# A two-layer encoder trunk in split fp32: low parts of two x forms made by DMA, a swapped pair of copies, an earlier weight split

## The chip, the cores and the metric

The kernel runs on one core of a Trainium2 chip. The metric is the device time of one execution in microseconds (us), as the median of several runs. Smaller is better. The engines are named as the profile names them: PE (matrix products; PEld is its weight loading), DVE (vector), ACT (scalar), POOL (GpSimd), SP (which here only starts transfers). Sixteen DMA engines move data for all queues; the profile calls the queue of transfers started by POOL q0 and the queue of those started by SP q1.

## The reference

Two layers run over x of 512 rows and 1024 columns. Each layer is a half-step SwiGLU FFN (hidden width 2816), a mixer, a second such FFN, and a gated embedding; each of these ends in a residual and a layer norm. The mixer of layer 0 is an mLSTM, that of layer 1 a gated MLP.

```
for i in range(DEPTH):
    x = layer_norm(DN_ALPHA*x + 0.5*swiglu_ffn(x, ffn1_wgu[i], ffn1_wd[i]), ...)
    x = layer_norm(DN_ALPHA*x + mixer(x), ...)          # mLSTM for i == 0, gMLP for i == 1
    x = layer_norm(DN_ALPHA*x + 0.5*swiglu_ffn(x, ffn2_wgu[i], ffn2_wd[i]), ...)
    x = layer_norm(DN_ALPHA*x + sigmoid(x @ ple_wg[i] + ple_bg[i]) * (p[i] @ ple_wp[i]), ...)

def swiglu_ffn(x, w_gu, w_d):
    g, u = split(x @ w_gu, 2); return (silu(g) * u) @ w_d
```

All inputs are float32, and the changed parts belong to `x @ w_gu` of the four FFNs and to the step from an FFN to the mixer behind it.

## The kernel before, in words

**Split products.** Every float32 operand is split in two fp32r tiles: a high part (the rounded value) and a low part (value minus high part). A product is three matmuls, high by high, high by low, low by high (`mm3`, L396, L397, L398 in the profile). So each weight tile passes ACT once for its high part (`whi`, L281), and its low part (`wlo`) is made in one of two ways:

- by DVE, as source minus high part (L290 or L296);
- by DMA: ACT writes the rounded value with its sign turned into the low tile (L287), and POOL starts a transfer that adds the source to it in place (L288, "DMA" `wlo<-wbox`). Both read the source; neither needs the high part.

**Seven products for eight.** Large products are done by a Strassen-like scheme. For the up projection of an FFN (`up_forms` for the weights, `UpForms` for x) four quarters of a pair of weight column blocks give seven weight forms, and the quarters of x give seven right-hand forms. The forms are numbered from 0 in the code and called first to seventh here. The fifth weight form (`s3`) and the third (`s2`) are sums that DVE makes in place in the loaded tile (L143 to L152); they are in the set `W.sums`. Which weight forms get their low part by DMA is in `UP_BY_DMA = (1, 3, 4, 5, 6)` for the first pair of each chunk, and in shorter lists for a chunk's second pair and for the last chunk. The fifth form (index 4) is in the first list only.

Of x, four forms are quarters as they stand and three are new: `t2` for the third product, `t1` for the fourth and `t4` for the seventh. A fourth sum, `t3`, replaces a quarter of x in place (the tiles `xh`, `xl`) and is used by the fifth product. `t2` already gets its low part by DMA. `t1`, `t3` and `t4` get theirs from DVE.

**Chunks.** An FFN's 22 hidden blocks run in chunks of 2, 4, 4, 4, 4 and 4 blocks. The first four blocks are plain products (`fps`, `sup`); the first pair by seven products is the second half of chunk 1. While its products run (`up_products`), the remaining x forms are made from the table `self.last`, one entry after each product: 0 splits `t3`, 1 and 2 make `t4`, 3 makes its high part, 4 its low part. After every second up product comes one product of the down projection (`gps`).

**What sets the order.** Each engine does its instructions in the order in which this code issues them. SP starts weight loads (L243) as soon as a raw tile comes free, that is when the last reader of the tile, often the transfer of a low part, is done. `W.fill` splits the next weights of a list when there is a free pair of tiles. `W.hold` keeps it from splitting a weight whose load was started less than two products ago; `W.limit` keeps it from going past the end of the FFN.

**The end of an FFN.** The down product of the last blocks (`down`, `dps`) runs over four blocks of 128 rows, with residual and norm behind each. PE transposes the finished rows of x (`xps`, L649), and ACT scales and splits them (`xf` L654, `xh` L657, low part on DVE L658; `turn_x`). Two blocks of rows are transposed within the next stage, between its first products (`sup`, `up_staged`, L888 and L892), which go over three weight tiles.

Of the kernel before, what the change touches and what calls it, by code (L numbers as in the profile page):

```python
# [10 lines left out]
F32 = mybir.dt.float32  # L11
F32R = mybir.dt.float32r
AF = mybir.ActivationFunctionType
OP = mybir.AluOpType
# [36 lines left out]
class Weights:  # L51
# [199 lines left out]
    def fill(self, most=1000, low=None, meanwhile=None):  # L251

        while most and self.next_split < len(self.order) and self.next_split != self.limit:
            kind, js, make = self.order[self.next_split]
            if not self.free.get(kind):
                return meanwhile
            for j in js or ():
                while j not in self.raws:
                    if not self.load(self.loads[j][1]):
                        return meanwhile  # L260
                if self.hold and self.ready and self.loaded_at[j] > self.clock - 2:
                    return meanwhile
            if self.ahead and not self.forced and make in self.sums and make not in self.made:
                return meanwhile
            shape = [P, 2, 512]
            if js is not None:
                while any(m not in self.formed for m in self.after.get(make, ())):
                    self.lows(1)
                src, used = self.made.pop(make, None) or make()
                shape = list(src.shape)  # L270
            hi = self.pools[kind].tile(shape, F32R, name="whi", tag="whi")
            lo = self.pools[kind].tile(shape, F32R, name="wlo", tag="wlo")
            self.free[kind] -= 1
            self.next_split += 1
            if js is None:
                make(hi, lo)
                continue
            parts = 2 if self.next_split == 1 else 1
            for i in range(parts):
                s = slice(i * shape[1] // parts, (i + 1) * shape[1] // parts)  # L280
                self.nc.scalar.activation(hi[:, s], src[:, s], AF.Copy)  # L281
                if meanwhile and make in self.in_place:
                    meanwhile()
                    meanwhile = None
                if make in self.by_dma or low == "dma" and make not in self.in_place:

                    self.nc.scalar.activation(lo[:, s], src[:, s], AF.Copy, scale=-1.0)  # L287
                    self.nc.gpsimd.dma_start(lo[:, s], src[:, s], accum_op=OP.add)  # L288
                elif not self.apart:
                    self.nc.vector.tensor_sub(lo[:, s], src[:, s], hi[:, s].bitcast(F32))  # L290
            self.ready.append((kind, (hi, lo)))
            most -= 1

            def done(make=make, used=used, src=src, hi=hi, lo=lo, late=self.apart and make not in self.by_dma):
                if late:
                    self.nc.vector.tensor_sub(lo, src, hi.bitcast(F32))  # L296
                self.formed.add(make)
                for j in used:
                    self.left[j] -= 1
                while self.load():  # L300
                    pass

            if self.apart and make not in self.by_dma:
                self.pending.append((lo, done))
            else:
                done()
        return meanwhile
# [58 lines left out]
def hybrid_trunk(ctx: ExitStack, tc, x, p, ln_g, ln_b, ffn1_wgu, ffn1_wd, ffn2_wgu, ffn2_wd,  # L366
# [3 lines left out]
    nc = tc.nc  # L370
# [21 lines left out]
    vec, sca, pool = nc.vector, nc.scalar, nc.gpsimd  # L392
# [7 lines left out]
    def split(hi, lo, src):  # L400
        sca.activation(hi, src, AF.Copy)
        vec.tensor_sub(lo, src, hi.bitcast(F32))
# [46 lines left out]
    W = Weights(nc, raw_pool, split_pool)  # L449
# [562 lines left out]
    class UpForms:  # L1012


        def __init__(self, pool, late):
# [3 lines left out]
            b, c = f32(pool, "f1"), f32(pool, "f0")  # L1019
# [7 lines left out]
            def f32r(to, at, tag):  # L1027
                to.append(at.tile([P, 4, 256], F32R, name="t_" + tag, tag=tag))
                return to[-1]
# [13 lines left out]
            def split_t1():  # L1043
                both = act.tile([P, 2, 4, 256], F32R, name="t1", tag="gb")
                self.t1.extend((both[:, 0], both[:, 1]))
                for i, s in enumerate(halves):
                    split(self.t1[0][:, s], self.t1[1][:, s], a[i])

            def split_t2():
                hi, lo = f32r(self.t2, late, "whi"), f32r(self.t2, late, "wlo")  # L1050
                sca.activation(lo, c, AF.Copy, scale=-1.0)
                nc.gpsimd.dma_start(lo, c, accum_op=OP.add)
                sca.activation(hi, c, AF.Copy)

            self.steps = [
                x22, lambda: joined(b, 0, 1), t3, lambda: joined(c, 0, 0), lambda: vec.tensor_add(c, b, c),
                split_t2, t1, split_t1]

            d = [tmp.tile([P, 2, 256], F32, name="x_d", tag="pad", bufs=3) for _ in range(2)]
# [14 lines left out]
            def t4_low():  # L1074
                lo = f32r(self.t4, pool, "f0")
                for i, s in enumerate(halves):
                    vec.tensor_sub(lo[:, s], d[i], self.t4[0][:, s].bitcast(F32))

            self.last = {0: lambda: split(*self.t3, b), 1: x21, 2: t4, 3: t4_high, 4: t4_low}
            self.right = [self.quarter(0, 0), self.quarter(1, 0), self.t2, self.t1, self.t3,  # L1080
                          self.quarter(1, 1), self.t4]

# [55 lines left out]
    def ffn(layer, k, rows, late, prepare=None):  # L1138
        with stage_pool("forms", 2) as fpool, stage_pool("quarters", Q_BUFS) as qpool, \
# [58 lines left out]
            for c, n in enumerate(FFN_CHUNKS):  # L1198
# [36 lines left out]
                else:  # L1235
# [3 lines left out]
                        next_group.form()  # L1239
                    group.add()  # L1240
                    group = next_group
            W.limit = None
            W.fill()
            W.apart, W.ahead, W.hold = (layer, k) == (0, 0), False, False
            return down(hs, False, norm, lazy=layer == 0, defer=prepare is not None)

    def ffn_stage(layer, k):
        with stage_pool("rows", 2) as rows, stage_pool("late") as late:
            W.open("rows", rows, 2)
            ffn(layer, k, rows, late)  # L1250
            W.close("rows")
            W.close("rowsx")
# [573 lines left out]
    def ffn_ple(i, last):  # L1826
        with stage_pool("rows", 2) as rows, stage_pool("late") as late:
# [3 lines left out]
            def load_p():  # L1831
# [13 lines left out]
                turn_p.append(turn)  # L1845

            finish = ffn(i, 2, rows, late, load_p)
            with stage_pool("extra", PLE_EXTRA) as extra, stage_pool("rows2") as rows2, stage_pool("ple2") as mp:
                W.open("extra", extra, PLE_EXTRA)
# [123 lines left out]
```

## Time and profile before

| | us |
|---|---|
| median of three runs (2177.74 to 2182.6) | 2177.97 |
| the profiled execution | 2179.46 |
| its span, first to last instruction | 2177.8 |
| PE busy in the span | 2161.0 |
| DVE busy | 1761.4 |
| ACT busy | 1244.9 |
| POOL busy | 253.8 |

The span is what the profile's rows add up to; the execution has 1.7 us more around it. The profiled execution is 1.5 us above the median. Busy shares are averages over stages that differ, and PE's busy time is that of pipelined matmuls, so the waits of PE, and what ended them, are read beside them.

### The profile page before, as it was taken

The numbers are of one execution on the slowest core, as the hardware profiler recorded it, in microseconds if no ns is written. First come the engines' busy times: TensorE is split into PE (matmuls) and PEld (weight loads), VectorE is DVE, ScalarE is ACT, GpSimd is POOL, SyncE is SP. The second block draws the span as 40 slices with busy tenths as digits, with TensorE's granted clock in tenths as the row PEclk, the third lists the DMA queues.
The fourth block names the chain that finished last, engine by engine and source line by source line (L and its number), as shares of the span: only waits on it lengthen the run. The fifth ranks groups of instructions, "written<-read, shape, count | busy, mean of one in ns | idle before, by whom it ended". The sixth has DMA issues, their size and how long they took to land. (4 is left out here: it accounts for less than half of the span.)

```text
span 2177.8 us, 33285 instructions
## 1 busy us (share of the span) xinstructions
PE 2161.0 (99%) x13109; PEld 1931.7 (89%) x13109; DVE 1761.4 (81%) x2540; ACT 1244.9 (57%) x1712; POOL 253.8 (12%) x311
## 2 busy tenths in 40 slices
PE   9999999999999999999999999999999999999998
PEld 8999998888888889999988999998888888999987
DVE  6988887777776789888887988887788678888897
ACT  4766656464646456666445666655345556666542
POOL 1111101011101111111000111100011101111100
PEclk9999999999999999999999999999999999999999
DMA  7887763366847468787544887763338748877651
GB/s 216 195 196 189 172 169 115 88 152 135 160 123 155 126 160 199 193 203 166 149 131 128 205 200 186 173 166 122 128 78 155 160 129 214 186 192 176 137 173 59
DMA packets 232836, 346.28 MB, mean 159 GB/s; under 512 B 9780, under 2 KB 164532, under 8 KB 232680
## 3 DMA queue, kind: packets, MB, share of 16 engines
q0 software_dynamic: 56832, 117.64, 31.8%
q1 hardware_dynamic: 169232, 211.83, 30.2%
q10 hardware_dynamic: 6616, 14.69, 2.0%
q8 instruction: 103, 1.69, 0.3%
q14 instruction: 53, 0.43, 0.1%
HBM read 224.58 MB, written 2.11 MB: 104 GB/s over the span
## 5 line engine op out<-in xcount | busy, mean ns | idle before, releaser
L281 ACT ACTIVATE whi<-wbox 128x1024 fp32r<-128x1024 f32 x252 | 265.1, 1054 | 239.9 <-DVE wbox L144 95.2
L398 PE MATMUL ups<-xh,wlo 128*128 128x256 f32 x1152 | 326.5, 283 | 4.3 <-DMA wlo<-wbox 4.3
L397 PE MATMUL ups<-xl,whi 128*128 128x256 f32 x1152 | 325.9, 283 | 0.0
L396 PE MATMUL ups<-xh,whi 128*128 128x256 f32 x1152 | 325.7, 283 | 0.0
L396 PE MATMUL gps<-whi,fhi 128*128 128x512 f32 x644 | 252.9, 393 | 0.0
L281 ACT ACTIVATE whi<-wraw 128x1024 fp32r<-128x1024 f32 (+1 forms) x196 | 200.5, 1045 | 90.8 <-DVE wraw L121 22.6
L397 PE MATMUL gps<-wlo,fhi 128*128 128x512 f32 x644 | 252.3, 392 | 0.0
L398 PE MATMUL gps<-whi,flo 128*128 128x512 f32 x644 | 251.5, 390 | 0.0
L288 POOL DMA_DIRECT2D wlo<-wbox x160 | 135.6, 848 | 945.5 <-ACT wlo L287 572.9
L398 PEld LDWEIGHTS ups<-xh,wlo 128*128 128x128 f32 x1152 | 220.7, 192 | 5.2 <-DMA wlo<-wbox 5.1
L397 PEld LDWEIGHTS ups<-xl,whi 128*128 128x128 f32 x1152 | 220.6, 192 | 2.6
L396 PEld LDWEIGHTS ups<-xh,whi 128*128 128x128 f32 x1152 | 220.6, 192 | 2.6
L784 DVE TENSOR_TENSOR xt<-xt,gps 128x512 f32<-128x512 f32 x302 | 195.6, 683 | 28.4 <-PE gps L398 28.3
L290 DVE TENSOR_TENSOR wlo<-wraw,whi 128x1024 fp32r<-128x1024 f32 (+1 forms) x120 | 143.5, 1213 | 38.1 <-ACT whi L281 37.2
L281 ACT ACTIVATE whi<-wquarter 128x1024 fp32r<-128x1024 f32 (+1 forms) x140 | 135.2, 966 | 56.4 <-ACT wlo L287 20.2
L287 ACT ACTIVATE wlo<-wbox 128x1024 fp32r<-128x1024 f32 x160 | 167.1, 1044 | 0.0
L398 PEld LDWEIGHTS gps<-whi,flo 128*128 128x128 f32 x644 | 120.9, 188 | 27.0
L396 PEld LDWEIGHTS gps<-whi,fhi 128*128 128x128 f32 x644 | 121.3, 188 | 22.0
L397 PEld LDWEIGHTS gps<-wlo,fhi 128*128 128x128 f32 x644 | 121.4, 188 | 21.3
L296 DVE TENSOR_TENSOR wlo<-wquarter,whi 128x1024 fp32r<-128x1024 f32 (+1 forms) x116 | 139.3, 1201 | 0.0
L970 DVE TENSOR_TENSOR flo<-h,fhi 128x512 fp32r<-128x512 f32 (+1 forms) x140 | 88.8, 637 | 44.6 <-ACT fhi L967 44.5
L967 ACT ACTIVATE fhi<-h 128x512 fp32r<-128x512 f32 (+1 forms) x140 | 80.4, 574 | 47.6 <-DVE h L1220 28.7
(367 smaller groups left out, 5814.7 us busy)
## 6 DMA issues: line engine op xcount, KB each, us to landing
wlo<-wbox POOLq DMA_DIRECT2D x160, 512.0 KB, 5.9
wbox<-in_ffn_wgu_dram SPq DMA_DIRECT2D x144, 512.0 KB, 4.6
wquarter<-in_ffn_wd_dram SPq DMA_DIRECT2D x64, 512.0 KB, 6.5
wraw<-in_ml_w_in_dram SPq DMA_DIRECT2D x24, 1024.0 KB, 5.7
wlo<-wraw POOLq DMA_DIRECT2D x48, 512.0 KB, 6.6
wraw<-in_gm_w_in_dram SPq DMA_DIRECT2D x15, 1024.0 KB, 5.9
wraw<-in_ffn_wgu_dram SPq DMA_DIRECT2D x17, 512.0 KB, 4.5
wraw<-in_ffn_wd_dram SPq DMA_DIRECT2D x8, 1024.0 KB, 5.0
```

Source lines behind the costliest of these rows:

```text
L281: self.nc.scalar.activation(hi[:, s], src[:, s], AF.Copy)
L287: self.nc.scalar.activation(lo[:, s], src[:, s], AF.Copy, scale=-1.0)
L288: self.nc.gpsimd.dma_start(lo[:, s], src[:, s], accum_op=OP.add)
L290: self.nc.vector.tensor_sub(lo[:, s], src[:, s], hi[:, s].bitcast(F32))
L296: self.nc.vector.tensor_sub(lo, src, hi.bitcast(F32))
L396: mm(ps, st[0], mv[0], start=start, stop=False, skip_group_check=more)
L397: mm(ps, st[0], mv[1], start=False, stop=False, skip_group_check=more)
L398: mm(ps, st[1], mv[0], start=False, stop=stop, skip_group_check=more)
L784: vec.tensor_add(dst, dst, ps)
L967: sca.activation(hi, src, AF.Copy)
L970: vec.tensor_sub(lo, src, hi.bitcast(F32))
```

## The change

There are four parts.

1. The low part of `t3` comes by DMA: ACT writes the negated copy into `xl`, POOL starts the adding transfer, then ACT writes `xh`. The DVE subtraction goes. A new helper `split_by_dma` does this for `t2` and `t3`.
2. The low part of `t4` comes by DMA too, in two halves, and is issued one entry earlier in the table (with the high part, after the fourth product). The two DVE subtractions go.
3. For a weight form that is a sum and whose low part comes by DMA (only the fifth form, in the first pair of each chunk), the negated copy and its transfer are issued before the high part.
4. `W.hold` is cleared before the `W.fill()` at the end of an FFN instead of after it.

```diff
+                by_dma = make in self.by_dma or low == "dma" and make not in self.in_place
+
+                def negated():
+                    self.nc.scalar.activation(lo[:, s], src[:, s], AF.Copy, scale=-1.0)
+                    self.nc.gpsimd.dma_start(lo[:, s], src[:, s], accum_op=OP.add)
+
+                if by_dma and make in self.sums:
+                    negated()
                 self.nc.scalar.activation(hi[:, s], src[:, s], AF.Copy)
...
-                if make in self.by_dma or low == "dma" and make not in self.in_place:
-
-                    self.nc.scalar.activation(lo[:, s], src[:, s], AF.Copy, scale=-1.0)
-                    self.nc.gpsimd.dma_start(lo[:, s], src[:, s], accum_op=OP.add)
-                elif not self.apart:
+                if by_dma and make not in self.sums:
+                    negated()
+                if not by_dma and not self.apart:
                     self.nc.vector.tensor_sub(lo[:, s], src[:, s], hi[:, s].bitcast(F32))
...
+            def split_by_dma(hi, lo, src):
+                sca.activation(lo, src, AF.Copy, scale=-1.0)
+                nc.gpsimd.dma_start(lo, src, accum_op=OP.add)
+                sca.activation(hi, src, AF.Copy)
+
             def split_t2():
-                hi, lo = f32r(self.t2, late, "whi"), f32r(self.t2, late, "wlo")
-                sca.activation(lo, c, AF.Copy, scale=-1.0)
-                nc.gpsimd.dma_start(lo, c, accum_op=OP.add)
-                sca.activation(hi, c, AF.Copy)
+                split_by_dma(f32r(self.t2, late, "whi"), f32r(self.t2, late, "wlo"), c)
...
             def t4_low():
                 lo = f32r(self.t4, pool, "f0")
                 for i, s in enumerate(halves):
-                    vec.tensor_sub(lo[:, s], d[i], self.t4[0][:, s].bitcast(F32))
-
-            self.last = {0: lambda: split(*self.t3, b), 1: x21, 2: t4, 3: t4_high, 4: t4_low}
+                    sca.activation(lo[:, s], d[i], AF.Copy, scale=-1.0)
+                    nc.gpsimd.dma_start(lo[:, s], d[i], accum_op=OP.add)
+
+            self.last = {0: lambda: split_by_dma(*self.t3, b), 1: x21, 2: t4, 3: lambda: (t4_high(), t4_low())}
...
-            W.limit = None
+            W.limit, W.hold = None, False
             W.fill()
-            W.apart, W.ahead, W.hold = (layer, k) == (0, 0), False, False
+            W.apart, W.ahead = (layer, k) == (0, 0), False
```

How this moves instructions: PE's and SP's rows keep their order. DVE loses three subtractions in each FFN, twelve in all.

ACT after the first up product of the second FFN, before the change. `us` is the copy of that product, `x_f` the tile of `t3`, the first `whi`, `wlo` are the fifth weight form, the second pair the sixth:

```order
L1114 ACTIVATE us<-ups 128x512
L401 ACTIVATE xh<-x_f_7664 128x4x256
L281 ACTIVATE whi<-wbox 128x1024
L287 ACTIVATE wlo<-wbox 128x1024
L281 ACTIVATE whi<-wbox 128x1024
L287 ACTIVATE wlo<-wbox 128x1024
```

The same place with the change (lines have moved: L284 is now the negated copy, L289 the high part):

```order
L1123 ACTIVATE us<-ups 128x512
L1056 ACTIVATE xl<-x_f_7667 128x4x256
L1058 ACTIVATE xh<-x_f_7667 128x4x256
L284 ACTIVATE wlo<-wbox 128x1024
L289 ACTIVATE whi<-wbox 128x1024 x2
L284 ACTIVATE wlo<-wbox 128x1024
```

A copy for `xl` has come in ahead of everything, and the fifth form's negated copy stands where it stood in the row, third after `us`; the sixth form's stands one copy later.

POOL from the end of the mLSTM stage to the end of the second FFN, before. The `wlo<-wbox` are the low parts of weight forms:

```order
L751 TENSOR_TENSOR rs<-rs,eps_pow 128x1 x4
L775 DMA xt<-gb 128x1024 x3
L288 DMA wlo<-wbox 128x1024
L775 DMA xt<-gb 128x1024
L1052 DMA t_wlo<-x_f_7665 128x1024
L288 DMA wlo<-wbox 128x1024 x39
L751 TENSOR_TENSOR rs<-rs,eps_pow 128x1 x8
```

With the change:

```order
L757 TENSOR_TENSOR rs<-rs,eps_pow 128x1 x4
L781 DMA xt<-gb 128x1024 x3
L285 DMA wlo<-wbox 128x1024
L781 DMA xt<-gb 128x1024
L1057 DMA t_wlo<-x_f_7668 128x1024
L285 DMA wlo<-wbox 128x1024
L1057 DMA xl<-x_f_7667 128x4x256
L285 DMA wlo<-wbox 128x1024 x3
L1086 DMA t_f_8137<-x_d 128x512 x2
L285 DMA wlo<-wbox 128x1024 x35
L757 TENSOR_TENSOR rs<-rs,eps_pow 128x1 x8
```

The transfer for `xl` has come in before those of the fifth, sixth and seventh weight form, and the two for `t4` (`t_f`) behind these three, ahead of the low part of the next chunk's second form.

ACT in the first products of the mLSTM stage, before. `xf` and `xh` are the last rows of x being turned, `whi` weights of the mLSTM, `pad` the first result of the stage:

```order
L654 ACTIVATE xf<-xps,cols 128x128 x4
L657 ACTIVATE xh<-xf 128x4x128
L281 ACTIVATE whi<-wraw 128x1024 x4
L654 ACTIVATE xf<-xps,cols 128x128 x4
L657 ACTIVATE xh<-xf 128x4x128
L654 ACTIVATE xf<-xps,cols 128x128 x4
L657 ACTIVATE xh<-xf 128x4x128
L1365 ACTIVATE pad<-sup,cols 128x512
```

With the change:

```order
L660 ACTIVATE xf<-xps,cols 128x128 x4
L663 ACTIVATE xh<-xf 128x4x128
L660 ACTIVATE xf<-xps,cols 128x128 x4
L663 ACTIVATE xh<-xf 128x4x128
L660 ACTIVATE xf<-xps,cols 128x128 x4
L663 ACTIVATE xh<-xf 128x4x128
L289 ACTIVATE whi<-wraw 128x1024 x3
L1374 ACTIVATE pad<-sup,cols 128x512
```

The four weight splits that stood ahead of the last two turned halves of x have left this place: one was done in the FFN's down product, three come behind the turned halves. The DVE low part of that one weight goes with it. At the start of the gMLP stage one of two such splits moves to the earlier place in the same way.

## The prediction

> **What bounds the kernel now.** I read the page first, then who PE waited for.
>
> ```profile
> span 2177.8 us, 33285 instructions
> PE 2161.0 (99%) x13109; PEld 1931.7 (89%) x13109; DVE 1761.4 (81%) x2540; ACT 1244.9 (57%) x1712; POOL 253.8 (12%) x311
> ...
> PEclk9999999999999999999999999999999999999999
> ...
> PE ups L398 <- DMA wlo<-wbox: 4.3, 4, 1.7
> ```
>
> PE is busy all but 17 us of the span, at full clock. So no change that leaves PE's work alone can gain more than about 0.7%, while what makes PE wait costs its whole length. The only repeated wait of PE is for low parts of weights that come by DMA, four times. They lie where this change works. The PE timeline of the second FFN and, as the fourth of them, of the last FFN:
>
> ```profile
> 822.50 0.39 PE L398 MATMUL ups<-xh,wlo 128*128 128x256 f32 x1 [0.70 <-DMA wlo<-wbox]
> 1852.10 0.39 PE L398 MATMUL ups<-xh,wlo 128*128 128x256 f32 x1 [0.53 <-DMA wlo<-wbox]
> ```
>
> The first is the fifth product (its matmul would have started 0.87 us earlier at the even step of 0.12 us), the second is the second product of the next chunk. Why these come late is seen in stretches of the second FFN. The last two columns are the DMA engines' busy share and GB/s:
>
> ```profile
> core 0: us, PE busy (x) PEld busy (x) DVE busy (x) ACT busy (x) POOL busy (x), PEclk, DMA share, GB/s
> ...
> 813.00:815.00 2.00, 2.00 (x13) 1.74 (x13) 2.00 (x5) 2.00 (x4) 0.00 (x0) 1.00 0.06 10
> 815.00:818.50 3.50, 3.50 (x32) 3.50 (x31) 3.50 (x6) 2.49 (x4) 1.70 (x2) 1.00 0.81 252
> 818.50:824.00 5.50, 4.80 (x35) 4.33 (x34) 5.04 (x9) 5.50 (x9) 0.86 (x1) 1.00 1.08 228
> 824.00:827.00 3.00, 3.00 (x27) 3.00 (x26) 1.50 (x2) 1.79 (x3) 0.00 (x0) 1.00 1.08 196
> 827.00:831.00 4.00, 4.00 (x30) 3.74 (x29) 2.93 (x5) 1.32 (x2) 0.84 (x1) 1.00 1.02 344
> 831.00:835.20 4.20, 4.20 (x37) 4.20 (x37) 3.69 (x5) 3.04 (x5) 0.00 (x0) 1.00 1.04 267
> 835.20:837.60 2.40, 2.40 (x22) 2.40 (x22) 2.40 (x5) 2.40 (x5) 0.85 (x1) 1.00 0.05 17
> ```
>
> From 815 to 835.2 the DMA engines are full; on both sides they idle. In these 20 us DMA, not DVE or ACT, sets when low parts arrive, and the last low part of the stretch is used at its end:
>
> ```profile
> 827.66 0.84 POOL L288 DMA_DIRECT2D wlo<-wbox  x1 [4.82 <-ACT wlo L287]
> ...
> wlo<-wbox POOLq DMA_DIRECT2D x1, 512.0 KB, 7.7
> ...
> 835.49 0.29 PE L398 MATMUL ups<-xh,wlo 128*128 128x256 f32 x1
> ```
>
> Issued at 827.66, landed 7.7 us later at 835.36, used at 835.49: 0.13 us of slack. The row of 1852.10 is this same low part in the last FFN, already late.
>
> **The order of transfers.** What decides the price of more DMA work is who goes first. A place with an alternating sequence: two low parts by POOL with a load by SP started between them, then the queues' shares in 189.5 to 192.3, 192.5 to 193.5 and 194 to 196:
>
> ```profile
> 186.73 0.84 POOL L288 DMA_DIRECT2D wlo<-wbox  x1 [7.17 <-ACT wlo L287]
> 187.60 0.37 SPq L243 DMA_DIRECT2D wquarter<-in_ffn_wd_dram  x1
> 189.63 0.85 POOL L288 DMA_DIRECT2D wlo<-wbox  x1 [2.06 <-ACT wlo L287]
> ...
> q0 software_dynamic: 121, 0.50, 91.4%
> ...
> q1 hardware_dynamic: 178, 0.36, 94.7%
> ...
> q0 software_dynamic: 102, 0.41, 103.6%
> ```
>
> The bytes go low part, load, low part, in the order of the starts: a load that was started earlier holds back a later low part, though another low part of the same queue is still under way. So I take the stretch as one line of work served in order of arrival.
>
> **Part 1, the low part of t3.** DVE loses one subtraction per FFN and ACT gets one copy. In the second FFN:
>
> ```profile
> 815.98 1.23 DVE L402 TENSOR_TENSOR xl<-x_f,xh 128x1024 fp32r<-128x1024 f32 x1
> ...
> 811.99 1.05 ACT L401 ACTIVATE xh<-x_f 128x1024 fp32r<-128x1024 f32 x1
> ...
> 813.89 1.04 ACT L287 ACTIVATE wlo<-wbox 128x1024 fp32r<-128x1024 f32 x1
> ...
> 815.23 0.86 POOL L288 DMA_DIRECT2D wlo<-wbox  x1 [5.31 <-ACT wlo L287]
> ...
> wlo<-wbox POOLq DMA_DIRECT2D x1, 512.0 KB, 7.2
> ```
>
> The 1.23 us of DVE buy nothing on PE: none of PE's rows at this place waits for DVE. The new copy starts at 811.99 where `xh` did, so POOL can start the transfer at about 813.3 (0.3 us behind ACT's end, as for the row at 815.23). Its work for the DMA engines: the destination has runs of 1 KB (256 columns), the source tile is whole. Two rows bound it, q0 alone in 822.2 to 824.6 (runs of 4 KB) and in 446.3 to 450.2 (runs of 512 B):
>
> ```profile
> q0 software_dynamic: 132, 0.48, 100.5%
> ...
> q0 software_dynamic: 1032, 0.54, 125.1%
> ```
>
> These are 0.48 MB in 2.4 us, so 2.6 us for 0.52 MB, and 3.9 us. I take 3.1, nearer the first, since a fixed cost per run weighs little at 1 KB; the bounds go to the range. Of the idle time before 815 it can use at most 1 us. POOL's issuing takes 0.84 us, so bytes cannot flow before 814.2 and hardly before the loads at 815: I take 0.2, which leaves 2.9 us ahead of the fifth low part. This low part, 815.23 plus 7.2, landed at 822.43, just ahead of PE's 822.50. So the fifth product waits longer, by up to 2.9 us.
>
> **Part 3, the swap.** The fifth form's negated copy stays the third ACT instruction behind `us`, at 813.89: `xl`'s copy takes the 1 us that the swap gives. Gain 0 in this stretch. In chunks 2 to 5 its transfer goes out 1 us earlier and its high part is done 1 us later; no PE row waits there for either, so 0. The sixth form's copy is 1 us later, hidden while its transfer stands in line behind the fifth's.
>
> **Part 2, the low part of t4.** DVE loses about 1.2 us, again not waited for. ACT gets two half copies behind `t_f`, 1.1 us by the high part's own row (2 x 128x512):
>
> ```profile
> 822.06 1.15 ACT L1072 ACTIVATE t_f<-x_d 128x512 fp32r<-128x512 f32 x2
> ```
>
> Behind them on ACT are the next chunk's splits, whose next wait is for PE's end of the fifth product, so this costs 0 by itself. POOL issues the halves at about 824, before the 827.66 row. Their work is 2.6 us at the 4 KB rate; with runs of 2 KB I take 2.7. They stand behind the seventh low part and ahead of the loads of 827 to 831 and of the low part used at 835.49. The seventh product needs them; it began at 829.5, so it too may wait, but that wait lies inside the total taken at 835.49.
>
> **The sum for one FFN.** Work put in ahead of the low part used at 835.49: 3.1 + 2.7 = 5.8 us. Less 0.2 idle used and 0.13 slack: 5.4 us later on PE, of which some 2.9 appears at the fifth product and the rest at the seventh and at the next chunk's second. This is the strict case. Once the line is longer, that low part may be ready while its loads still queue, and pass one of them; one load of 0.52 MB is 1.4 us at the rate of 827.3 to 831:
>
> ```profile
> DMA packets 1161, 1.35 MB, mean 365 GB/s; under 512 B 47, under 2 KB 960, under 8 KB 1161
> ```
>
> That gives 4.0. I take the middle, 4.7, and for all four FFNs the same: they run the same rows. 4 x 4.7 = 18.8 us. Nothing gives it back: behind 835.2 DMA is idle, but PE is at 99% and cannot catch up.
>
> **Part 4, the earlier split.** At the start of the mLSTM stage:
>
> ```profile
> 353.01 3.89 ACT L281 ACTIVATE whi<-wraw 128x1024 fp32r<-128x1024 f32 x4
> 356.80 1.49 ACT L654 ACTIVATE xf<-xps,cols 128x128 f32<-128x128 f32 x4
> ...
> 359.01 0.38 PE L888 MATMUL sup<-xh,whi 128*128 128x256 f32 x1 [0.24 <-ACT xh L657]
> 361.07 0.39 PE L888 MATMUL sup<-xh,whi 128*128 128x256 f32 x1 [0.84 <-ACT xh L657]
> ```
>
> Four weight splits (3.89 us) run ahead of the last turned halves, and PE then waits. With them behind, the halves come as soon as PE has transposed them, and both waits (0.24 and 0.84, or 0.44 and 1.05 on the weight loading) go: a gain of 1.4 us, between 0 and 1.6. The split that moves into the down product costs 1.05 us of ACT where ACT idles, and 1.2 of DVE. At the gMLP's start no PE wait stands, gain 0.
>
> **Sum.** +18.8 - 1.4 = +17.4 us on the profiled 2179.46. Against the median of 2177.97, which is 1.5 us lower, that is 2195.4; I say 2195, 0.8% slower. Own range of this case 2188 to 2201: four strict FFNs with a `t3` price of 3.9 give 4 x 6.2 - 1.4 = +23.4 (2201), four FFNs of 2.9 (the `t3` term alone) give +10 (2188).
>
> **Rivals.** (a) The queues share instead of standing in line. For it: in 824 to 827, with a low part and a load started half a us apart, both moved:
>
> ```profile
> q0 software_dynamic: 125, 0.48, 94.3%
> q1 hardware_dynamic: 106, 0.11, 13.6%
> ```
>
> If they shared so all through, loads would fall back (they are split only in the next chunk) and low parts hardly: `xl`'s 3.1 us, in runs as short as the load's, stretch to some 4.5, the fifth low part's 2.6 to 3.0, so from 815 its bytes end at 822.5 and it lands about 1 us later than now; `t4`, counted on in the same way, adds about 0.5. That is 4 x 1.5 - 1.4 = +4.6, or 2182.6. Against it: the three stretches at 189.5 to 196, and q1's hold on 815 to 818.5. [...]
>
> (b) The work fits: `xl`'s bytes use the idle 1 us and the loads behind are not needed in order, so PE's waits stay. Then only part 4 counts: 2176.6. Against it: slack of 0.13 us.
>
> (c) Faster: the fifth low part lands earlier, the four waits of 4.3 us go, and with part 4 the kernel gains 5.7, or 2172.3. It decides at 822.43: the landing must come 0.9 us sooner in the second FFN. It would need the negated copy ahead of 813.89, and ACT's order excludes that unless `xl`'s copy starts earlier.
>
> **Chances.** Line in order of arrival, 2188 to 2201: 0.63. (a) 0.2, (b) 0.09, (c) 0.03, dearer than 2201: 0.05. A difference within 0.3%, 6.5 us, can't be told from none here: 2171.4 to 2184.5 is "same". That takes (b), (c) nearly all, and most of (a): same 0.27, slower 0.71, faster 0.02. The range for 8 in 10 goes from 2181, which takes in (a), to 2202.
>
> **What would show it.** Right: at the fifth product of each FFN a PE wait for `wlo<-wbox` of 2 to 4 us, a shorter one at the seventh product (for `t_f`) or at the next chunk's second, full DMA from 814 to about 841 in the second FFN, and no wait at 359 and 361. Wrong: the fifth product's wait no longer than now, or gone; `xl`'s transfer landing later than the fifth low part; or loads (`wbox`, `wquarter`) becoming what PE or ACT waits for.

## The result and the profile after

The changed kernel takes 2197.2 us (median of 6 runs, 2196.26 to 2198.87) against 2178.28 us for the kernel before in the same session (6 runs, 2177.74 to 2182.6): 18.9 us slower, a ratio of 1.0082 with a 95% interval of 1.0071 to 1.0093. The profiled execution took 2197.1 us, its span is 17.6 us longer than before (2195.4 against 2177.8).

The page after, its first lines and PE's two largest waits:

```profile
span 2195.4 us, 33303 instructions
...
PE 2169.7 (99%) x13109; PEld 1938.9 (88%) x13109; DVE 1752.0 (80%) x2528; ACT 1252.5 (57%) x1724; POOL 265.7 (12%) x323
...
PE ups L404 <- DMA wlo<-wbox: 9.8, 6, 2.5
PE ups L403 <- DMA xl<-x_f: 4.0, 3, 2.2
```

The number of matmuls is the same and so is their work, but PE is *busy* for 8.7 us longer, and it waits for low parts by DMA for 13.8 us where it waited for 4.3. The wait for turned halves of x (`sup`) has left the list. The place where both losses arise, in the second FFN: PE's timeline at the fifth product, then stretches (columns as in the prediction: busy time of each engine, granted clock, DMA share, GB/s):

```profile
825.30 0.38 PE L403 MATMUL ups<-xl,whi 128*128 128x256 f32 x1 [0.80 <-DMA xl<-x_f]
827.77 0.58 PE L404 MATMUL ups<-xh,wlo 128*128 128x256 f32 x1 [2.08 <-DMA wlo<-wbox]
```

```profile
819.00:824.00 5.00, 5.00 (x40) 4.78 (x40) 4.91 (x9) 5.00 (x8) 0.84 (x1) 1.00 1.10 257
824.00:828.00 4.00, 1.12 (x5) 0.60 (x4) 1.41 (x3) 3.44 (x7) 1.53 (x3) 0.84 1.10 216
828.00:832.00 4.00, 4.00 (x20) 4.00 (x21) 0.00 (x0) 0.50 (x1) 1.04 (x2) 0.50 1.06 205
832.00:836.00 4.00, 4.00 (x29) 4.00 (x29) 1.82 (x2) 2.95 (x3) 0.84 (x1) 0.80 1.09 261
836.00:842.70 6.70, 6.70 (x53) 6.44 (x51) 4.19 (x4) 2.09 (x4) 0.00 (x0) 1.00 1.05 303
```

First the fifth product waits, for `xl` and then for its weight's low part. Then comes what the prediction had not thought of: behind the wait the granted clock falls to 0.50, and in 828 to 832 PE does 20 matmuls where it does some 30. In the trace's record of the clock these stretches last 3.413 us each, one in the first, third and fourth FFN and two in a row in the second. A matmul that follows its neighbour after 0.120 us at full clock follows it after 0.213 us there, so a full stretch of 16 matmuls costs 1.5 us. Matched matmul by matmul, the timelines of the two profiled executions give the loss by place:

- the fifth product's wait: 1.9, 2.4, 2.4 and 2.9 us more in the four FFNs, 9.7 in all;
- the half clock behind it: 1.6, 2.5, 1.5 and 1.5 us, 7.1 in all (in the second FFN PE still stood waiting for the first 1.0 us of its two stretches), which is most of the 8.7 us of added busy time;
- the rest: +2.0 at three later products, -0.6 for a wait that has gone in the last FFN, -1.4 at the start of the mLSTM stage, +0.8 in small steps elsewhere.

The sum is 17.6. Taken by FFN, the four lose 4.1, 5.0, 4.1 and 5.0 us, 18.1 in all.

The matmul that the prediction read at 835.49, in the next chunk's second product, and the one at 361.07, in the mLSTM stage, now start here, without a wait for DMA or ACT:

```profile
843.30 0.28 PE L404 MATMUL ups<-xh,wlo 128*128 128x256 f32 x1
...
363.92 0.39 PE L894 MATMUL sup<-xh,whi 128*128 128x256 f32 x1
```

Of the delay of 7.81 us at the first, 2.83 stood there when the second FFN began, so this FFN lost 5.0.

Transfers in the same FFN: the starts on POOL and SP, the queues' shares in 817.6 to 819 (one row, q0 has none) and in 819.5 to 824 (two rows), and the time to landing of `xl` and of the fifth low part:

```profile
816.16 1.29 POOL L1057 DMA_DIRECT2D xl<-x_f  x1 [3.41 <-DVE wlo L296]
818.05 0.88 POOL L285 DMA_DIRECT2D wlo<-wbox  x1 [0.60 <-ACT wlo L284]
...
816.71 0.37 SPq L243 DMA_DIRECT2D wbox<-in_ffn_wgu_dram  x1
817.17 0.46 SPq L243 DMA_DIRECT2D wquarter<-in_ffn_wd_dram  x1
...
q1 hardware_dynamic: 215, 0.22, 70.3%
...
q0 software_dynamic: 466, 0.48, 65.9%
q1 hardware_dynamic: 454, 0.69, 47.5%
...
xl<-x_f POOLq DMA_DIRECT2D x1, 512.0 KB, 9.1
...
wlo<-wbox POOLq DMA_DIRECT2D x1, 512.0 KB, 9.7
```

`xl`'s transfer starts where the prediction put it (813.3 plus the 2.83 us brought along is 816.13), but its bytes do not go first: up to 819 the loads move alone, then both share, and `xl` lands at 825.26, where PE stands waiting. The fifth low part, which would need 2.6 us by the prediction's estimate from its 4 KB row, lands 9.7 us after its start.

### The profile page after: what moved, and what is told of

It reads as the page before. It is cut to its first block, busy times and chain, and to the rows that moved or that the text cites. A ratio compares the mean times of both kernels' runs of the same rounds, so it can differ in the third digit from the quotient of the medians.

```text
span 2195.4 us, 33303 instructions
## 1 busy us (share of the span) xinstructions
PE 2169.7 (99%) x13109; PEld 1938.9 (88%) x13109; DVE 1752.0 (80%) x2528; ACT 1252.5 (57%) x1724; POOL 265.7 (12%) x323
## 5 line engine op out<-in xcount | busy, mean ns | idle before, releaser
L289 ACT ACTIVATE whi<-wbox 128x1024 fp32r<-128x1024 f32 x252 | 264.2, 1053 | 239.1 <-DVE wbox L144 109.8
L289 ACT ACTIVATE whi<-wraw 128x1024 fp32r<-128x1024 f32 (+1 forms) x196 | 200.5, 1045 | 90.6 <-DVE wraw L121 22.6
L284 ACT ACTIVATE wlo<-wbox 128x1024 fp32r<-128x1024 f32 x160 | 167.3, 1046 | 11.4 <-DVE wbox L152 11.4
L289 ACT ACTIVATE whi<-wquarter 128x1024 fp32r<-128x1024 f32 (+1 forms) x140 | 135.2, 966 | 56.7 <-ACT wlo L284 20.4
```

## Experiments: what the clock costs, and what the transfers cost

Two theories stood after the result. **L**: the transfers form a line of work, and the line sets when the next products can go on; the half clock only fills time in which PE would have waited later. **C**: the loss is the fifth product's wait plus the half clock, and what stands behind in the line costs nothing. All times below are medians against runs of the kernel before on the same chip in the same session.

| kernel | difference, us | ratio, 95% interval | clock of the profiled run |
|---|---|---|---|
| changed kernel | +18.9 | 1.0082 [1.0071, 1.0093] | 0.995 |
| t3_only | +14.7 | 1.0068 [1.0053, 1.0083] | 0.997 |
| t3_busy | +10.7 | 1.0046 [1.0032, 1.0060] | 0.999 |
| t4_only | +12.6 | 1.0056 [1.0041, 1.0071] | 0.995 |
| t4_busy | +10.6 | 1.0050 [1.0036, 1.0064] | 0.999 |
| keep_busy | +16.7 | 1.0076 [1.0061, 1.0091] | 0.999 |
| seventh_by_dve | +14.9 | 1.0063 [1.0048, 1.0078] | 0.995 |
| keep_busy_seventh | +10.9 | 1.0048 [1.0032, 1.0065] | 0.999 |
| weight_first_after | +19.9 | 1.0090 [1.0075, 1.0106] | 0.996 |

A clock of 0.999 is that of the kernel before: no stretch at half clock but the one in which the kernel ends (there from 2171.24 us on).

### Each transfer alone

t3_only is the kernel before with part 1 alone:

```
-            self.last = {0: lambda: split(*self.t3, b), 1: x21, 2: t4, 3: t4_high, 4: t4_low}
+            self.last = {0: lambda: split_by_dma(*self.t3, b), 1: x21, 2: t4, 3: t4_high, 4: t4_low}
```

> The kernel before with part 1 alone: t3's low part comes by DMA, nothing else is changed. Theory L (a line of DMA work): the time is set by how much transfer work stands ahead of the next chunk's second low part; t3 alone puts 2.6 to 3.9 us per FFN in line, less 0.2 of idle time: 4 x 2.9 = about +11 us against the kernel before (+9 to +14), whether or not the clock falls. Theory C (waits at the fifth product and the half-clock stretches behind them, as the changed kernel's trace has them): PE's waits there grow by 9.4 us and five stretches of 3.41 us at half clock cost 8.5, and t4's transfer, which comes behind, adds nothing: about +18 us.

Measured +14.7: between the two. Its waits of PE:

```profile
PE ups L398 <- DMA wlo<-wbox: 9.5, 4, 3.1
PE ups L397 <- DMA xl<-x_f: 3.7, 3, 1.6
```

The fifth product waits, three half-clock stretches follow, and no product behind waits. So t3's transfer alone costs more than its place in the line.

t4_only is the kernel before with part 2 alone:

```
-                    vec.tensor_sub(lo[:, s], d[i], self.t4[0][:, s].bitcast(F32))
+                    sca.activation(lo[:, s], d[i], AF.Copy, scale=-1.0)
+                    nc.gpsimd.dma_start(lo[:, s], d[i], accum_op=OP.add)
...
-            self.last = {... 3: t4_high, 4: t4_low}
+            self.last = {... 3: lambda: (t4_high(), t4_low())}
```

> The kernel before with part 2 alone: t4's low part comes by DMA. Its transfer is issued behind the fifth product, so nothing of it can lengthen the fifth product's wait. Theory L: 2.7 us per FFN stand ahead of the next chunk's second low part, which has 0.13 us of slack in the second FFN: +8 to +11 us, as waits at the seventh product (for t_f) or the next chunk's second product, and no half clock needed. Theory C: 0 to +2 us, no new waits of more than 0.5 us.

Measured +12.6: theory C, by which it costs nothing, falls; L's place is right, its upper bound of 11 is passed by 1.6, and half clock is there too. The four runs differ in how much of it they have: 2189.54 and 2191.06 us at a mean clock of 0.998, 2193.74 and 2194.15 at 0.996 and 0.995. The seventh product of the second FFN, and the starts of two loads and of the first half of its transfer:

```profile
836.05 0.58 PE L397 MATMUL ups<-t_f,whi 128*128 128x256 f32 x1 [3.59 <-DMA t_f<-x_d]
...
825.07 0.37 SPq L243 DMA_DIRECT2D wbox<-in_ffn_wgu_dram  x1
...
827.65 0.84 POOL L1078 DMA_DIRECT2D t_f<-x_d  x1 [1.19 <-ACT t_f L1077]
...
827.76 0.37 SPq L243 DMA_DIRECT2D wbox<-in_ffn_wgu_dram  x1
```

The transfer for `t_f` starts 2.6 us behind one load of SP and 0.1 us ahead of the next. In the changed kernel it starts ahead of both (the second starts at 830.21):

```profile
827.32 0.84 POOL L1086 DMA_DIRECT2D t_f<-x_d  x1 [1.85 <-ACT t_f L1085]
...
827.78 0.37 SPq L243 DMA_DIRECT2D wbox<-in_ffn_wgu_dram  x1
```

There the first load is late, for it waits for the transfer of the fifth low part, the last reader of the tile that it fills: this landed at 827.75, 0.03 us ahead of the load, and in t4_only the load starts at 825.07. So one load less stands ahead of `t_f`. This is one reason why the two transfers together cost less (18.9, with part 4's gain in it) than the sum of each alone (27.3); the half clock, which both single numbers hold, is another.

### The same with PE kept busy

Dummy transposes ahead of the product at which PE waits fill the wait with activity. In the changed kernel (keep_busy):

```
                     if r == 0:
                         pair = UpPair(formed, None if h is None else h[:, b:b + 2])
+                    if plain and r == 4:
+                        warm({(0, 0): 12, (0, 2): 24, (1, 0): 30, (1, 2): 37}[layer, k])
                     pair.product(r)
```

> The changed kernel, with dummy transposes of PE ahead of chunk 1's fifth product in each FFN (12, 24, 30 and 37 of about 0.11 us: 1.3, 2.6, 3.3 and 4.1 us, about as long as PE waits there), so that PE does not stand idle; their results are not used. The granted clock should then stay at 1.0 behind the fifth product. Theory C: the five stretches at half clock were 8.5 us of the loss, so the time falls by about 8 us against the changed kernel. Theory L: the same transfers stand in line, so what the full clock saves comes back as waits at the seventh product and the next chunk's second product: 0 to -2 us.

Measured +16.7: 2.2 us under the changed kernel by the differences, 0.7 by the medians themselves (2196.53 and 2197.2), and neither can be told from nothing by the two intervals. The clock did stay up; stretches of the second FFN and PE's waits:

```profile
824.00:828.00 4.00, 2.88 (x27) 2.67 (x24) 1.03 (x2) 2.98 (x6) 1.43 (x3) 1.00 1.09 215
828.00:832.00 4.00, 3.74 (x31) 3.74 (x32) 0.73 (x2) 1.46 (x2) 1.13 (x2) 1.00 1.06 209
...
PE ups L404 <- DMA wlo<-wbox: 5.2, 6, 1.9
PE ups L403 <- DMA t_f<-x_d: 2.9, 4, 0.8
```

31 matmuls in 828 to 832, not 20, and little or nothing won: PE now waits at the seventh product for `t_f`, in all four FFNs, and at the next chunk's second product for `wlo`, in three. This is the picture that the prediction had drawn, but for the longest wait, 1.90 us, which comes later still, at chunk 2's seventh product in the second FFN. Matched with the kernel before, keep_busy loses 4.3, 6.7, 4.1 and 3.2 us in the four FFNs, 18.2 in all, where the changed kernel loses 18.1. So in the changed kernel the half clock stands in place of these later waits, and theory C's 8.5 us (7.1 by the timeline) are no loss of their own there.

Whether that holds with one transfer alone, t3_busy tells (t3_only with the same edit, counts 12, 26, 32, 33):

> t3's low part by DMA alone, as in t3_only (14.7 us slower than before), and the dummy transposes of PE ahead of chunk 1's fifth product in each FFN (13, 26, 32, 33 counted as 12, 26, 32, 33 of 0.11 us; results not used), about as long as PE waits there. t3_only had three stretches of 3.41 us at half clock, 1.65 us of loss each, and no wait at the seventh product or the next chunk's second behind them. Theory C (with t3 alone the half clock is a loss of its own): about -5 us against t3_only, i.e. +9 to +10 against before. Theory L (the line of transfers sets when the next chunk can go on, whatever the clock): what the clock saves comes back as waits behind the fifth product, +13 to +15 against before.

Measured +10.7, 4.0 us under t3_only: C's account holds here (its number was 9 to 10), since behind t3 alone little else is late. And t4_busy (t4_only, dummies ahead of the seventh product 20, 38, 26, 3, ahead of the fifth in the last two FFNs 3 and 17):

> t4's low part by DMA alone, as in t4_only (+12.6 us against before, with four stretches at half clock, one of them twice as long), and dummy transposes of PE where it waits there: ahead of chunk 1's seventh product in the four FFNs 20, 38, 26 and 3, ahead of its fifth product in the last two 3 and 17, of 0.11 us each; results not used. Theory of the sum (at full clock the two transfers add up, 2.7 us per FFN for t3 as measured, and what is left of the changed kernel's 16.9 with part 4's -1.4 taken out, 7.6, for t4): about +7.6 against before, and t4_only's other 5 us were half clock. Rival: what the full clock saves comes back as waits behind the seventh product, as it did in the changed kernel with dummy transposes: +11 to +13.

Measured +10.6, 2.0 under t4_only; 7.6, which the sum wanted, was missed, and the rival's 11 to 13 is not far. The 2.0 us are uncertain: the runs of the two kernels overlap, and the two runs of t4_only at a clock of 0.998 are no slower than t4_busy (2190.14 to 2191.96). So some of the half clock was a loss of its own; that the rest came back as waits is argued, not shown. The waits that are left:

```profile
PE ups L397 <- DMA t_f<-x_d: 3.1, 4, 1.4
```

In both kernels one FFN shows no wait left behind the dummies (the third in t3_busy, the second in t4_busy), so there they may have been too long, and the two numbers are upper bounds of what the transfers cost at full clock.

### Less work behind

seventh_by_dve takes 2.6 us of transfer out of the line behind the fifth low part:

```
-                                            by_dma=UP_BY_DMA if b == starts[c] + plain else ...
+                                            by_dma=(1, 3, 4, 5) if plain else UP_BY_DMA if b == starts[c] + plain else ...
```

> The changed kernel with chunk 1's seventh weight form's low part computed by DVE instead of by DMA, and no dummy transposes: 2.6 us less transfer work per FFN behind the fifth low part, the waits and half-clock stretches at the fifth product as in the changed kernel. With dummy transposes the same edit gave -5.8 us. Theory of two limits that run side by side (the time is the later of the half-clock products and the transfers behind them): 0 to -2 us against the changed kernel, since the half clock stays. Theory L alone: about -6 us, as with the full clock.

keep_busy_seventh has this edit and the dummies of keep_busy:

> The same dummy transposes, and chunk 1's seventh weight form has its low part computed by DVE instead of by DMA: 2.6 us less transfer work per FFN between the fifth low part and the next chunk's second. If both limits hold at once (the time is the later of the two), taking away both gives about -8 us against the changed kernel, though either alone gives little. Theory C alone: also about -8, all of it from the clock. Theory L alone: about -10 from the seventh low part, nothing from the clock.

Measured +14.9 and +10.9. The first is 4.0 less than the changed kernel, between the numbers of two limits and of L alone. The second is 8.0 less than the changed kernel, the number of two limits (and of C), and 5.8 less than keep_busy. Waits of seventh_by_dve, then of keep_busy_seventh:

```profile
PE ups L404 <- DMA wlo<-wbox: 10.2, 4, 4.3
PE ups L403 <- DMA xl<-x_f: 3.2, 2, 1.8
```

```profile
PE ups L404 <- DMA wlo<-wbox: 4.6, 6, 1.3
...
PE ups L403 <- DMA t_f<-x_d: 0.8, 1, 0.8
```

With the line shortened behind, no product behind the fifth waits in seventh_by_dve, and the half clock is what is left: keeping PE busy is now worth 4.0 us by the differences, where it was worth 2.2 with the full line. The intervals do not separate these two, but the timelines of the one profiled execution of each kernel point the same way: in the four FFNs together seventh_by_dve loses 16.5 us and keep_busy_seventh 13.8, while the changed kernel and keep_busy lose the same. So both limits are there and, as far as this shows, run side by side: behind the fifth product the time is the later of PE at half clock and the transfers. What the shorter line gave at full clock, 5.8 us, is less than the 10.4 us of work (4 x 2.6) taken out of it; why is open.

### The order in the line

swap_split is the kernel before with parts 3 and 4 alone (the edits of the change without the lines of t3 and t4):

> The kernel before with parts 3 and 4 alone (the fifth form's negated copy ahead of its high part; the next stage's weights split at the end), t3's and t4's low parts by DVE as before. By the prediction's steps part 4 gives -1.4 us; part 3, with xl's new copy not in its way, puts the fifth low part's transfer out 1 us earlier. Theory 1: the transfer then comes ahead of a load of SP that stood ahead of it, the fifth product's waits (4.3 us in all) go: -4 to -5.7 us against before. Theory 2: the load is still ahead, the transfer only waits longer in line: -1.4 us. No stretch at half clock in either.

2177.33 against 2179.6 us (21 runs): -2.3 us by the medians, -1.7 by the ratio of 0.9992 [0.9983, 1.0001], an interval that just takes in no change; theory 2. In the timelines 1.4 us of it are at the start of the mLSTM stage (part 4) and 1.0 in the last FFN. The starts in the second FFN and PE's wait:

```profile
812.94 0.86 POOL L285 DMA_DIRECT2D wlo<-wbox  x1 [4.37 <-DVE t L408]
...
812.67 0.37 SPq L243 DMA_DIRECT2D wbox<-in_ffn_wgu_dram  x1
...
PE ups L404 <- DMA wlo<-wbox: 3.0, 4, 1.1
```

Part 3 does put the transfer out 1 us earlier, and misses the load by 0.27 us. In 814.5 to 817.5 the loads then move alone:

```profile
q1 hardware_dynamic: 580, 0.76, 86.5%
```

weight_first moves the transfer past the load:

```
-                    if plain and s in formed.last:
+                    if plain and s in formed.last and s:
                         formed.last[s]()
                     W.release()
+                    if plain and s == 0:
+                        formed.last[0]()
```

> swap_split, and t3's split (xh by ACT, xl by DVE) called behind the release that splits the fifth weight form, so that the fifth form's negated copy comes ahead of xh on ACT and its transfer can go out about 1 us earlier again: at about 812.0 in the second FFN, where SP starts its two loads at 812.67 and 813.13. Theory of the line: the low part is now ahead of these loads (1 MB, some 3 us of DMA time), so PE's waits at the fifth product (1.04, 1.35, 1.23 us in three FFNs) go, and DMA engines that idled from 811 to 813.5 are used: -3 to -4 us against swap_split, -5 to -6 against before. Rival: the loads' bytes still come first, or xl's later subtraction on DVE makes PE wait in its place: as swap_split or slower.

2176.89 against 2179.88: ratio 0.9986 [0.9978, 0.9995], -3.0 us. Starts, the queues' shares in 813 to 815.5, and PE's wait:

```profile
811.46 0.86 POOL L285 DMA_DIRECT2D wlo<-wbox  x1 [3.42 <-DVE wlo L296]
...
812.73 0.37 SPq L243 DMA_DIRECT2D wbox<-in_ffn_wgu_dram  x1
...
q0 software_dynamic: 99, 0.41, 109.5%
...
PE ups L404 <- DMA wlo<-wbox: 2.7, 3, 1.4
```

The low part goes ahead of the loads: q0 is full from 813 on, at most 1.5 us after the start on POOL, where in swap_split q0 has no row up to 817.5, 4.6 us after the start, so there the loads held it back for some 3 us (an estimate from these two). The fifth product no longer waits in any FFN (in swap_split 1.0, 0.4 and 1.2 us in the last three; a further 1.0 that the expectation counted in is the sixth product's). But only a part of it stays: in the last two FFNs the sixth product now waits 1.5 and 1.2 us, for the next low part in the line.

The same edit on the changed kernel (weight_first_after):

> The changed kernel with the same edit: the fifth weight form's transfer is issued ahead of xl's. Theory of the line: the fifth low part uses 1 to 2.5 us in which the DMA engines idle, and is ahead of SP's two loads; xl's transfer comes behind these loads and sets the fifth product's wait. The work behind the idle time shrinks by 1 to 2.5 us per FFN: 4 to 8 us faster than the changed kernel, still slower than before. Rival: only the order in the line changes, the waits go from wlo to xl: 0 to -2 us.

Measured +19.9, no better than the changed kernel: my expectation fell, the rival holds. The wait goes over to what now stands behind the loads:

```profile
PE ups L403 <- DMA xl<-x_f: 15.0, 4, 5.2
PE ups L403 <- DMA t_f<-x_d: 5.1, 5, 1.6
```

Two transfers are wanted at one product. In the second FFN the fifth low part's (started at 816.90) goes ahead of the loads of 817.56 and 818.02, and `xl`'s (818.79) stands behind them.

low_last leaves the line alone and asks for the low part later; swap_split with this in `product`:

```
+            if self.low_last and r == 4:
+                for i, j in ((0, 0), (0, 1), (1, 0)):
+                    for e in range(2):
+                        for k in range(4):
+                            mm(ps[:, e], w[i][:, k, e * P:(e + 1) * P], self.right[r][j][:, k], start=False,
+                               stop=i == 1 and k == 3, skip_group_check=True)
+                return
```

> swap_split, and in chunk 1's fifth product the eight matmuls that need the weight's low part come last of the 24 (high by high, high by x's low part, low by high), so that the low part is needed some 1.9 us later. A landing that is late by up to 1.8 us then costs nothing: PE's waits at the fifth product go in all four FFNs whichever theory of swap_split holds: -4 to -6 us against before (2172 to 2174 where before is 2178). Rival: the waits move to the next chunk's second product, as the line of transfers is as long as it was: -1.4 to -3.

2177.94 against 2179.6, 0.9990 [0.9981, 0.9999]: no better than swap_split: the rival. The fifth product still waits once, 0.8 us, and the sixth now waits in all four FFNs, 0.5 to 1.5 us; in the second:

```profile
825.43 0.39 PE L404 MATMUL ups<-xh,wlo 128*128 128x256 f32 x1 [1.31 <-DMA wlo<-wbox]
```

Both together, with the order of low_last in the fifth and the sixth product (`r in (4, 5)`), is weight_first_low_last:

> weight_first (3 us faster than before), and in chunk 1's fifth and sixth product the eight matmuls that need the weight's low part come last of the 24, so that these low parts are needed some 1.9 us later. weight_first still waits 1.5 and 1.2 us at the sixth product of two FFNs and 0.5 us once at the seventh. If the line has room behind (DMA engines idle from the next chunk's second low part on), these waits go: -2 to -2.7 us against weight_first, -5 to -6 against before. Theory of the line, as low_last showed it: the waits move on to the seventh product or the next chunk's second, whose low parts stand behind in the same line: 0 to -1 against weight_first.

2175.47 against 2179.89 us: ratio 0.9979 [0.9970, 0.9988], -4.4 us. This version beats both kernels. Its gain over weight_first (1.4 us by the medians) is less than the noise of the two comparisons; the waits went down from 2.7 to

```profile
PE ups L404 <- DMA wlo<-wbox: 1.9, 3, 0.9
```

and are all at the seventh product, one further.

## Why the prediction was right, and where it was not

The total was right, 2195 against 2197.2 us, and so was the kind of reason: more transfer work in a stretch that had no room. Its steps:

- **t3's price**, 3.1 us of work per FFN, 2.9 less the idle time: in the changed kernel's second FFN the 512 packets of `xl`'s transfer take 3.2 us of the 16 engines (some 0.10 us a packet of 1 KB; how much a run of 1 KB costs was my estimate between the two rows), and t3_busy has 10.7 / 4 = 2.7 at full clock.
- **t4's price**, 2.7 us per FFN: the 256 packets of `t_f`'s transfer take 2.8 us, and t4_busy has 10.6 / 4 = 2.65. These are averages: by the timelines the four FFNs of t3_busy lose 2.6, 4.2, 2.7 and 1.9 us and those of t4_busy 3.0, 3.4, 3.7 and 1.0. In t4_busy's second and third FFN the fifth product's wait of the kernel before (0.9 and 1.6 us) is not there and the seventh product loses more; that its mean comes out at 2.65 is partly luck.
- **The sum**, 5.4 strict, 4.0 with a load passed, 4.7 taken: the FFNs lose 18.1 us in the changed kernel and 18.2 in keep_busy, 4.5 and 4.6 per FFN. The 0.7 us that the two terms do not add up to is there; the rows show `t_f`'s transfer ahead of a load that it stands behind when it comes alone. I had thought of a low part that passes a load, not of `t_f`, and had taken the middle between two cases; that it fits so well is luck. That this order makes the 0.7 was not tried by itself.
- **Where it appears.** This failed. I put 2.9 us at the fifth product and the rest at the seventh or the next chunk's second. In the changed kernel nearly all of it, 16.8 of 18.1 us, is spent by the end of the half clock behind the fifth product's wait, 9.7 as wait and 7.1 as half clock, and the later waits are missing but for 2.0 us at three products. (The wait for `wlo` at the fifth product, for which I had named 2 to 4 us, is 1.8 to 2.5 in the trace's rows.) The step that failed is the silent one that matmuls go at one pace: the kernel before, with waits of up to 1.7 us and the clock at 1.00 behind them, gave no sign of it. keep_busy shows the later waits where I had them. The total was safe only since the line was at least as long as the half clock; with less behind it, as in t3_only, seventh_by_dve or t4_only, the half clock adds 2 to 4 us that my steps do not hold.
- **`xl` ahead of the loads, using 0.2 us of idle time**: wrong. The loads' bytes moved first, and `xl` landed at 825.26, later than its matmuls wanted it, so that the fifth product waits twice. It still landed 2.5 us before the fifth low part (825.26 against 818.05 + 9.7 = 827.75), so the order of the two low parts was as I had it. The mistake changes what PE is said to wait for, not the sum.
- **Part 3, 0**: right in the changed kernel (the fifth low part starts at 818.05, which is 815.23 plus the 2.83 brought along). Without `xl`'s copy it is 1 us earlier, as swap_split shows, and still behind the load.
- **Part 4, -1.4**: right. Between the first FFN and the second the delay drops by 1.4 us in the changed kernel, and in swap_split too, and the page's wait of `sup` for `xh` is gone.
- **Rival (a)**, queues that share, 2182.6: excluded by the time. The rows of 819.5 to 824 do show both queues moving, q0 with 65.9% and q1 with 47.5%. In 817.6 to 819 the load moved alone (q1 70.3%), though `xl`'s transfer had been issued at 816.16; whether the load held it back no run here tells. The low part of swap_split was held back, for some 3 us, and there the queues did not share. What the rival had wrong is the conclusion: where both move, the fifth low part behind them is about as late as if they moved one by one (the fifth product of the second FFN waits 2.4 us more, where the line had up to 2.9).
- **Rival (b)**, the work fits, 2176.6: excluded by the time.
- **Rival (c)**, the fifth low part ahead: it did not happen, for the reason given. weight_first, without the two new transfers, puts the negated copy where this rival wanted it, and that gives -3.0, not -5.7: the next low part in the line is late then.

## What to carry to other kernels

Price a transfer in a full stretch by its work (bytes over the rate seen for its shape; here 512 KB took 3.2 us in packets of 1 KB and 2.8 in packets of 2 KB), and trust the sum more than the place: who waits changed with every edit here, while the changed kernel and keep_busy lost the same. The sum is no law, though: work taken out of the line gave back about half of its price. Before moving work onto DMA look for where the engines idle and whether the transfer can start there, ahead of the loads; in swap_split a transfer that missed a load by 0.3 us waited for it and for the next. And a wait of PE of some 2 us can cost more when nothing behind it is late: in t3_only each of the three stretches of slower matmuls (0.213 us apart for 0.120, by the changed kernel's trace) cost 1.3 us, by its 4.0 us over t3_busy.

## What was not expected of the hardware

The clock fell behind waits that left PE some work in between. Three waits: the first FFN of the changed kernel, whose clock fell; the last FFN of the kernel before and the first FFN of t3_only, whose clock stayed up:

```profile
78.74 0.38 PE L404 MATMUL ups<-xh,wlo 128*128 128x256 f32 x1 [1.77 <-DMA wlo<-wbox]
...
1838.41 0.39 PE L398 MATMUL ups<-xh,wlo 128*128 128x256 f32 x1 [1.66 <-DMA wlo<-wbox]
...
78.47 0.39 PE L398 MATMUL ups<-xh,wlo 128*128 128x256 f32 x1 [2.01 <-DMA wlo<-wbox]
```

So 1.77 us of idle PE were followed by 3.413 us at half clock, and 1.66 and 2.01 us were not: length alone does not decide it. In the record of the clock the half-clock stretches of the changed kernel's four FFNs start at 79.23, 826.75, 1232.94 and 1854.16 us, which lie 219, 119 and 182 times 3.413 us apart. Counted in the same steps, in each kernel from a half-clock stretch of its own record, the stretches around the three waits, in the same order:

```profile
75.82:79.23 3.41, 1.64 (x10) 1.26 (x10) 1.38 (x2) 3.12 (x6) 1.74 (x3) 1.00 1.07 211
79.23:82.65 3.42, 3.42 (x19) 3.42 (x18) 0.00 (x0) 0.18 (x1) 0.72 (x1) 0.50 1.06 211
...
1836.74:1840.15 3.41, 1.75 (x15) 1.74 (x15) 1.76 (x3) 2.37 (x4) 0.84 (x1) 1.00 1.07 210
...
74.11:77.52 3.41, 2.35 (x15) 1.88 (x13) 2.07 (x4) 2.86 (x5) 0.83 (x1) 1.00 1.14 225
77.52:80.94 3.42, 2.47 (x20) 2.47 (x21) 0.00 (x0) 0.59 (x1) 0.00 (x0) 1.00 1.08 213
```

The 1.77 us lie in one such stretch, which has PE busy for 1.64 us; the 1.66 us lie in one too, with 1.75 us of work. The 2.01 us fall into two stretches, and each still has some 2.4 us of work. In the traces of the kernel before and the changed kernel the stretches at full clock with the most idle PE have 2.45, 2.31, 1.86 (twice), 1.77 and 1.66 us of it: half clock followed on the first two, on one of the two with 1.86 and on the one with 1.77, and on none with less. That the work in such a stretch decides is my reading of these rows; no run moved a wait from one stretch into two to test it. Dummy transposes of 0.11 us each (in the changed kernel ten of them at 7.95 us take 1.25 us), about as many as fill the wait, went with a mean clock of 0.999 in all four kernels that had them.
